# Five dense chunks at the head of the value pass, and the list constants on GpSimd in three blocks

## The chip, the cores and the metric

The kernel runs on one core of a Trainium2 chip. The metric is the device time of one launch in microseconds (us), the median of the runs shown. Five engines work side by side, each on its own queue in order: PE (matmuls), DVE (vector), ACT (activations and casts), POOL (GpSimd; here it also issues every indirect DMA) and SP (issues plain DMAs). The profile's names for them are used throughout; PEld is PE's weight load.

## The reference

A decoder trunk of two layers on 256 tokens of width 1024. Each layer is a token mixer (mLSTM in layer 0, RG-LRU in layer 1) with a memory cross-attention beside it, a layer norm, and then a channel mixer called PEER, whose second half is what matters here. PEER scores 128 x 128 = 16384 experts by products of two keys, keeps 16 experts for each of 8 heads and each token, and computes

```python
u = u_tab[eid]
act = jax.nn.gelu(jnp.einsum('nhkd,nd->nhk', u, xb).astype(jnp.float32), approximate=False)
coef = (gw * act).astype(x.dtype)
return jnp.einsum('nhk,nhkd->nd', coef, v_tab[eid])
```

A second layer norm follows. All arrays are float32.

## The kernel before

**Precision.** Every large product is made of three matmuls (`mm3`, lines 253 to 257): operands are split into a high part (a cast on ACT, line 153 for weights, 310 for coefficients) and a low part (a subtraction, line 163, 166 or 168 on POOL or DVE for weights, 311 on DVE for coefficients), and high x high, high x low and low x high are added in PSUM. The split of weights is called `wH`, `wL`; that of coefficients `cH`, `cL`. Both have rings of three buffers (`HL_BUFS`), so the cast for one chunk waits until PE has finished the chunk three places ahead of it.

**PEER as dense tables.** The 16384 experts lie in 128 chunks of 128. In the U pass, `u_step` multiplies chunk after chunk of the U table with all 256 tokens (24 matmuls of 128x256 in each step); GELU and the routing weights give a coefficient for each expert and token, in the tiles `lo` (chunks 0 to 47, tile name `wglo`) and `hi` (chunks 48 to 127, `wghi`). The first 48 steps run beside the routing, the next 64 beside the building of the routing weights, and the last 16 (`h` = 64 to 79, lines 1450 to 1467) beside a generator, `tail_lists`, that is advanced once for each step.

**Lists.** Of chunks 0 to 103 (`NJ` = 104) few rows matter, since each token uses 128 experts. `lists` (from line 1079) finds for each of the 128 partitions which chunks hold a used expert, and packs the used rows into 54 columns: 16 + 5 that matter only for the first block of 128 tokens, 16 + 6 only for the second, and 11 for both (columns 21 to 31). The results are `vrow` (`vids`: which rows of the V table a column needs) and `crow` (which rows of the coefficients, which the kernel dumps to a DRAM tensor `rows`, line 1073). The first 11 of its pieces are eleven `tensor_reduce` on DVE, counted by `tick`; at tick 4, POOL makes index constants (lines 1120 to 1137) in a part of `lo` that is free by then. Chunks 104 to 127 are dense: all their rows are used, and their coefficients are on the chip.

**Value pass.** It adds up 78 items: 24 dense chunks and 54 sparse columns. For an item of both blocks of tokens PE runs 12 matmuls of 128x512, for a column of one block 6. `value_order` (lines 66 to 86) fixes the order of the items from three numbers: it models that the first column can be multiplied at `FIRST_US`, one more every `PAIR_US`, that a dense item takes `ITEM_US`, and places dense chunks wherever a column would still be late. The last 3 items of layer 0 and the last 6 of layer 1 are kept apart and multiplied for the first block of tokens, then for the second.

**What a column needs.** A dense chunk is loaded by SP (line 200) into one of 5 `raw` buffers, or into one of 9 further buffers of the same size that come free in the pass (`ahead` in `wghi`, and `slots`). A column needs two indirect DMAs that POOL issues (line 205): a gather of 128 rows of V (512 KB) into such a buffer, and a gather of its coefficient rows (`wghi<-rows,crow`) into `hi`. As soon as `vids` is there, `begin` (line 208) issues gathers for the first five columns, and `coef_rows` (line 1436) issues coefficient gathers up to ten items ahead, four at a time. All of it stands in POOL's one queue in program order. `load` (line 176) takes the items in order and stops at a column while `vids` is not known.

The numbers behind the order:

```python
FIRST_US, PAIR_US, ITEM_US = 5.0, 2.8, 2.73
...
        while dense and t < FIRST_US + k * PAIR_US:
            out.append((dense.pop(0), None))
            t += ITEM_US
        t = max(t, FIRST_US + k * PAIR_US) + ITEM_US * len(blocks(c)) / 2
```

With them the order of layer 0 begins D D 21 0 D 1 2 D 3 22 (D a dense chunk, a number a column).

Of the kernel before, what the change touches and what calls it, by code (L numbers as in the profile page):

```python
# [39 lines left out]
COLS = A_END + SIDE + SPILLS[1]  # L40
WIDTH = 57
NC = P - NJ + COLS
FIRST_US, PAIR_US, ITEM_US = 5.0, 2.8, 2.73
SLOTS = 4
CLASS = 128.0
SKEW = 3
# [49 lines left out]
class Trunk:  # L96
# [982 lines left out]
    def lists(self, layer):  # L1079
        nc = self.nc  # L1080
# [3 lines left out]
        def take(*shape, dt=F32):  # L1084
            n = math.prod(shape)
            w = n if dt is not F16 else (n + 1) // 2
            v = words[:, at[0]:at[0] + w]
            at[0] += w
            assert at[0] <= 20 * T
            v = v if dt is F32 else v.bitcast(dt)  # L1090
            if len(shape) == 2:
                v = v.rearrange("p (a b) -> p a b", a=shape[0])
            return v
# [6 lines left out]
        pi, qi, ti, zi = take(3, NJ, dt=I32), take(2, dt=I32), take(4, dt=I32), take(SPILL, dt=I32)  # L1100
        jv, pq, tv, zv = take(3, NJ), take(4), take(4), take(SPILL)
# [15 lines left out]
        for tick, g in enumerate(g for g in range(NJ // 8) if g not in ACT_GROUPS):  # L1117
            nc.vector.tensor_reduce(mB[:, 8 * g:8 * g + 8], self.part_of(8 * g, 8, 1), axis=AX.X, op=ALU.max,
                                    apply_absolute_value=True)
            if tick == 4:  # L1120
                g_ = nc.gpsimd
                g_.iota(pi, pattern=[[int(CLASS), 3], [1, NJ]], base=1, channel_multiplier=0)
                g_.iota(qi, pattern=[[-P, 2]], base=1, channel_multiplier=1)
                g_.iota(ti, pattern=[[int(CLASS), 4]], base=0, channel_multiplier=0)
                g_.iota(zi, pattern=[[P, SPILL]], base=0, channel_multiplier=0)
                g_.tensor_copy(jv, pi)
                g_.tensor_copy(pq[:, 0:2], qi)
                for c in (1, 2):
                    g_.tensor_scalar(pq[:, 1 + c:2 + c], pq[:, 1:2], -CLASS * P * c, None, op0=ALU.add)
                g_.tensor_copy(tv, ti)  # L1130
                g_.tensor_copy(zv, zi)
                g_.memset(one, 1.0)
                g_.affine_select(tri, one, pattern=[[1, P]], base=0, channel_multiplier=-1,
                                 compare_op=ALU.is_gt, fill=0.0)
                g_.memset(ones, 1.0)
                for c in range(3):
                    g_.memset(zoff[:, first[c]:first[c + 1]], -P - CLASS * P * c)
            if tick == 8:
                b = self.bank()
                jp, tp = b[:, :3 * NJ].rearrange("p (a b) -> p a b", a=3), b[:, 3 * NJ:3 * NJ + 4]  # L1140
                nc.scalar.copy(jp, jv)
                nc.scalar.copy(tp, tv)
            yield 1.15
# [120 lines left out]
    def peer_layer(self, layer):  # L1264
        nc, tc, A = self.nc, self.tc, self.A
        with ExitStack() as ctx:
# [123 lines left out]
            def tail_lists():  # L1390
                lists = self.lists(layer)
                marks = [c for g in ACT_GROUPS for c in range(8 * g, 8 * g + 8)]
                budget, n = 0.0, 0
                while True:
                    gain = LIST_US if self.vrow is None else REST_US
                    budget = min(budget + gain, gain)
                    if n < NJ // 8:
                        self.dump(nc.scalar, 8 * DUMPS[n], 8, CUT, T)
                    while lists and budget > 0:
                        c = next(lists, -1.0)  # L1400
                        if c is None:
                            break
                        if c < 0:
                            lists = None
                            break
                        budget -= c
                    for _ in range(3):
                        if marks:
                            self.used(marks.pop(0), 1)
                    self.marked = not marks  # L1410
                    self.dumped = n >= NJ // 8 - 1
                    self.listed = not lists
                    n += 1
                    yield
# [286 lines left out]
```

## Time and profile before

| | |
|---|---|
| median of 3 runs | 1483.71 us (1479.94 to 1486.09) |
| the profiled execution: time, span | 1483.08 us, 1481.3 us |
| PE busy | 1438.8 us (97% of the span) |
| DVE, ACT, POOL busy | 1191.7, 892.2, 683.1 us |
| last 16 U steps | about 544 to 588 us in layer 0, 1262 to 1306 us in layer 1 |
| value pass on PE | 588.49 to 752.3 us in layer 0, 1306.49 to 1473.2 us in layer 1 |
| indirect DMAs issued by POOL | 108 in each layer |

Times in the profile are microseconds from the start of the span. A timeline row gives start, duration, engine, line, operation, the tile written and the tiles read, and in brackets how long the engine sat idle ahead of it and what ended the wait ("issue" means nothing that the profile shows). A row with "x6" merges six instructions that follow one another. A waits row gives the total of the waits, how many there were, and the longest. A windows row gives the stretch, its length, the busy time and count of each engine asked for, the granted TensorE clock as a share of full speed, the busy share of the DMA engines and GB/s.

### The profile page before, as it was taken

How to read it: one execution, taken by the hardware profiler on the slowest of the kernel's cores; microseconds unless marked ns; L12 is line 12 of the kernel's file. 1: busy time of each engine (PE TensorE's matmuls, PEld its weight loads, DVE VectorE, ACT ScalarE, POOL GpSimd, SP SyncE). 2: the span in 40 equal slices, each digit the busy share in tenths (PEclk: the TensorE clock that was granted, in tenths of full speed). 3: DMA queues.
4: the chain of work that ended last, by engine and by line, in shares of the span. 5: the costliest groups of instructions: out<-in, count | busy, mean ns of one | idle time of the engine just before them, and what ended most of it. 6: DMA issues, size and time to landing. Idle time of an engine off the chain costs nothing.

```text
span 1481.3 us, 30314 instructions
## 1 busy us (share of the span) xinstructions
PE 1438.8 (97%) x11173; PEld 1355.4 (91%) x11173; DVE 1191.7 (80%) x2688; ACT 892.2 (60%) x1895; POOL 683.1 (46%) x571
## 2 busy tenths in 40 slices
PE   9999999999999999899999999999999999989997
PEld 8998999999999999688899789999999999978885
DVE  4677377989999998687886855979899999777777
ACT  5555455455559984477756645555455798636664
POOL 2202578213333348777710166732333333877772
PEclk9999999999999999999999999999999999999999
DMA  7645655555548999889855255555555799988982
GB/s 235 228 141 172 202 172 185 186 179 163 167 161 270 263 244 279 305 291 324 285 203 176 72 174 171 173 186 171 185 158 164 225 277 259 257 301 286 312 282 87
DMA packets 165787, 317.41 MB, mean 214 GB/s; under 512 B 65245, under 2 KB 94946, under 8 KB 165378
## 3 DMA queue, kind: packets, MB, share of 16 engines
q1 hardware_dynamic: 90552, 226.68, 47.5%
q0 software_dynamic: 19360, 65.16, 13.1%
q10 hardware_dynamic: 55722, 23.60, 6.0%
q8 instruction: 88, 1.44, 0.4%
q14 instruction: 65, 0.53, 0.1%
HBM read 287.07 MB, written 28.32 MB: 213 GB/s over the span
## 4 chain that ended last, share of the span: by engine, by line
PE 35%; issue 5%; POOL 4%; DVE 3%; DMA 3%; ACT 1%; DVEq 0%; POOLq 0%; ACTq 0%
PE bank L255 11%; PE bank L257 11%; PE bank L256 11%; POOL wghi L205 2%; PE bank L1374 2%; DMA wghi<-in_v_dram,vids 1%; DMA wghi<-rows,crow 1%; DVE wL L168 1%; POOL raw L205 1%; PE bank L314 1%; DMA slots<-in_v_dram,vids 1%; POOL slots L205 0%; DVE xc L829 0%; ACT pr L545 0%; ACT wH L153 0%
## 5 line engine op out<-in xcount | busy, mean ns | idle before, releaser
L255 PE MATMUL bank<-xHL,wH 128*128 128x256 f32 x2536 | 716.8, 283 | 1.8 <-ACT wH L153 1.8
L257 PE MATMUL bank<-xHL,wL 128*128 128x256 f32 x2536 | 706.5, 279 | 9.1 <-DVE wL L168 6.2
L256 PE MATMUL bank<-xHL,wH 128*128 128x256 f32 x2536 | 704.6, 278 | 2.3 <-DVE xHL L311 2.2
L153 ACT CAST wH<-raw 128x1024 fp32r<-128x1024 f32 (+3 forms) x409 | 421.6, 1032 | 392.1 <-PE bank L256 124.1
L257 PEld LDWEIGHTS bank<-xHL,wL 128*128 128x128 f32 x2536 | 476.4, 188 | 13.3 <-DVE wL L168 9.1
L255 PEld LDWEIGHTS bank<-xHL,wH 128*128 128x128 f32 x2536 | 477.6, 188 | 3.0 <-ACT wH L153 2.8
L256 PEld LDWEIGHTS bank<-xHL,wH 128*128 128x128 f32 x2536 | 477.3, 188 | 3.1 <-DVE xHL L311 3.1
L166 POOL TENSOR_TENSOR wL<-raw,wH 128x1024 fp32r<-128x1024 f32 (+1 forms) x123 | 271.1, 2210 | 193.9 <-ACT wH L153 191.7
L168 DVE TENSOR_TENSOR wL<-raw,wH 128x1024 fp32r<-128x1024 f32 (+3 forms) x194 | 210.4, 1090 | 146.7 <-ACT wH L153 144.6
L163 POOL TENSOR_TENSOR wL<-raw,wH 128x386 fp32r<-128x386 f32 x128 | 131.4, 1027 | 285.4 <-DVE wL L161 285.4
L255 PE MATMUL bank<-wH,cH 128*128 128x512 f32 (+1 forms) x443 | 174.7, 394 | 12.3 <-ACT cH L310 12.0
L257 PE MATMUL bank<-wH,cL 128*128 128x512 f32 (+1 forms) x443 | 174.1, 393 | 0.0
L256 PE MATMUL bank<-wL,cH 128*128 128x512 f32 (+1 forms) x443 | 173.8, 392 | 0.0
L1027 DVE TENSOR_TENSOR oh<-iota,i12T 128x1024 f16<-128x1024 f16 x128 | 136.3, 1065 | 0.0
L205 POOL DMA_INDIRECT wghi<-rows,crow x108 | 118.6, 1098 | 32.9 <-issue 30.8
L255 PEld LDWEIGHTS bank<-wH,cH 128*128 128x128 f32 x443 | 84.4, 191 | 31.7 <-ACT cH L310 13.7
L161 DVE TENSOR_TENSOR wL<-raw,wH 128x640 fp32r<-128x640 f32 x128 | 105.5, 824 | 9.1 <-ACT wH L153 3.2
L257 PEld LDWEIGHTS bank<-wH,cL 128*128 128x128 f32 x443 | 84.2, 190 | 18.4 <-DVE cL L311 0.6
L256 PEld LDWEIGHTS bank<-wL,cH 128*128 128x128 f32 x443 | 84.3, 190 | 17.8 <-DVE wL L168 0.2
L1030 DVE TENSOR_TENSOR oh<-oh,gT 128x1024 f16<-128x1024 f16 x128 | 90.0, 703 | 4.4
L168 DVE TENSOR_TENSOR wL<-wghi,wH 128x1024 fp32r<-128x1024 f32 x56 | 68.5, 1223 | 25.0 <-ACT wH L153 25.0
L153 ACT CAST wH<-wghi 128x1024 fp32r<-128x1024 f32 x56 | 58.8, 1050 | 36.9 <-PE bank L257 35.7
(373 smaller groups left out, 2017.6 us busy)
## 6 DMA issues: line engine op xcount, KB each, us to landing
raw<-in_u_dram SPq DMA_DIRECT2D x256, 512.0 KB, 3.4
raw<-in_w_q_dram SPq DMA_DIRECT2D x32, 512.0 KB, 3.8
raw<-in_v_dram SPq DMA_DIRECT2D x21, 512.0 KB, 4.8
wghi<-in_v_dram SPq DMA_DIRECT2D x17, 512.0 KB, 4.8
raw<-in_w_out_dram SPq DMA_DIRECT2D x16, 512.0 KB, 3.8
rows<-wghi ACTq DMA_DIRECT2D x14, 512.0 KB, 5.7
rows<-wglo ACTq DMA_DIRECT2D x12, 512.0 KB, 4.4
slots<-in_v_dram SPq DMA_DIRECT2D x10, 512.0 KB, 6.0
```

The lines of the kernel that those rows point to most:

```text
L153: (nc.vector.tensor_copy if self.cast_dve else nc.scalar.copy)(h[:, c], r[:, c])
L161: nc.vector.tensor_sub(l[:, k:], r[:, k:], h[:, k:].bitcast(F32))
L163: nc.gpsimd.tensor_sub(l[:, :k], r[:, :k], h[:, :k].bitcast(F32))
L166: nc.gpsimd.tensor_sub(l[:, :k], r[:, :k], h[:, :k].bitcast(F32))
L168: nc.vector.tensor_sub(l[:, k:], r[:, k:], h[:, k:].bitcast(F32))
L205: self.nc.gpsimd.indirect_dma_start(out=dst, out_offset=None, in_=table, in_offset=bass.IndirectOffsetOnAxis(ap=rows, axis=0))
L255: mm(out, sH, mH, start=start, stop=False, skip_group_check=True)
L256: mm(out, sH, mL, start=False, stop=False, skip_group_check=True)
L257: mm(out, sL, mH, start=False, stop=stop, skip_group_check=True)
L1027: nc.vector.tensor_tensor(flat(oh[:, 1:3]), self.iota2.unsqueeze(1).to_broadcast([P, 4, P, 2]), pairs(self.i12T[:, j]), op=ALU.is_equal)
L1030: nc.vector.tensor_tensor(flat(oh[:, 0:2]), two.rearrange("p z (q e t) -> p z q e t", q=2, t=2), pairs(self.gT[:, j]), op=ALU.mult)
L1374: nc.tensor.matmul(wp[:, qs], oh[:, 2, q // 2, :, q % 2], oh[:, z, q // 2, :, q % 2], start=z == 0, stop=z == 1, skip_group_check=True)
```

## The change

Two constants of `value_order` are new, and POOL's constants for the lists are made at ticks 4, 6 and 8 in place of all at tick 4. Two ticks fall in one U step, so the three blocks stand beside three U steps that follow one another.

```diff
-FIRST_US, PAIR_US, ITEM_US = 5.0, 2.8, 2.73
+FIRST_US, PAIR_US, ITEM_US = 13.0, 2.65, 2.73
...
+            g_ = nc.gpsimd
             if tick == 4:
-                g_ = nc.gpsimd
                 g_.iota(pi, pattern=[[int(CLASS), 3], [1, NJ]], base=1, channel_multiplier=0)
+                g_.iota(ti, pattern=[[int(CLASS), 4]], base=0, channel_multiplier=0)
+                g_.tensor_copy(jv, pi)
+                g_.tensor_copy(tv, ti)
+            if tick == 6:
                 g_.iota(qi, pattern=[[-P, 2]], base=1, channel_multiplier=1)
-                g_.iota(ti, pattern=[[int(CLASS), 4]], base=0, channel_multiplier=0)
                 g_.iota(zi, pattern=[[P, SPILL]], base=0, channel_multiplier=0)
-                g_.tensor_copy(jv, pi)
                 g_.tensor_copy(pq[:, 0:2], qi)
                 for c in (1, 2):
                     g_.tensor_scalar(pq[:, 1 + c:2 + c], pq[:, 1:2], -CLASS * P * c, None, op0=ALU.add)
-                g_.tensor_copy(tv, ti)
                 g_.tensor_copy(zv, zi)
+            if tick == 8:
                 g_.memset(one, 1.0)
```

The order of layer 0 now begins D D D D D 21 0 D 1 2 D 3 22. The three dense chunks come from later places: the dense chunk behind column 5, one behind column 37 and one behind column 20 are gone from there. From column 48 on the two orders are the same, and so is the amount of work: 24 dense chunks, 54 columns, 678 matmuls in each layer's pass.

POOL's queue in the last U steps of layer 0, before (`wL<-raw,wH` is the subtraction of one U step, `wglo` the place of the constants):

```order
L166 TENSOR_TENSOR wL<-raw,wH 128x1024 x3
L1122 IOTA wglo 128x312
L1123 IOTA wglo 128x2
L1124 IOTA wglo 128x4
L1125 IOTA wglo 128x14
L1126 CAST wglo<-wglo 128x312
...
L1133 AFFINE_SELECT wglo<-wglo 128x128
...
L1137 MEMSET wglo 128x3
L166 TENSOR_TENSOR wL<-raw,wH 128x1024 x10
```

and now, at the same place:

```order
L166 TENSOR_TENSOR wL<-raw,wH 128x1024 x3
L1122 IOTA wglo 128x312
L1123 IOTA wglo 128x4
L1124 CAST wglo<-wglo 128x312
L1125 CAST wglo<-wglo 128x4
L166 TENSOR_TENSOR wL<-raw,wH 128x1024
L1127 IOTA wglo 128x2
...
L1132 CAST wglo<-wglo 128x14
L166 TENSOR_TENSOR wL<-raw,wH 128x1024
L1134 MEMSET wglo 128x128
...
L1139 MEMSET wglo 128x3
L166 TENSOR_TENSOR wL<-raw,wH 128x1024 x8
```

Thirteen subtractions stand there in both (3 + 10, and 3 + 1 + 1 + 8); two of them have moved ahead of parts of the constants. Some rows of constants are left out of both.

POOL's queue behind it, where the gathers of layer 0 begin, before (`vids` gathers fetch V rows, `crow` gathers coefficient rows):

```order
L205 DMA wghi<-in_v_dram,vids 128x1024 x5
L205 DMA raw<-in_v_dram,vids 128x1024
L205 DMA wghi<-rows,crow 128x256
L205 DMA wghi<-rows,crow 128x128 x3
L205 DMA raw<-in_v_dram,vids 128x1024
L205 DMA wghi<-rows,crow 128x128
```

and now:

```order
L205 DMA wghi<-in_v_dram,vids 128x1024 x5
L205 DMA wghi<-rows,crow 128x256
L205 DMA wghi<-rows,crow 128x128 x3
L205 DMA slots<-in_v_dram,vids 128x1024 x4
L205 DMA raw<-in_v_dram,vids 128x1024
L205 DMA wghi<-rows,crow 128x128
```

The first coefficient gather is now the sixth of the queue, where it was the seventh; the number of gathers is 108 in both.

ACT's queue at the head of the value pass of layer 0, before (`wH` is the cast of an item, `cH` that of its coefficients two items ahead of PE):

```order
L1455 ACTIVATE bank<-bank 128x256 x2
L153 CAST wH<-wghi 128x1024
L310 CAST cH<-wghi 128x256
L153 CAST wH<-wghi 128x1024
L310 CAST cH<-wghi 128x128
```

and now:

```order
L1457 ACTIVATE bank<-bank 128x256 x2
L153 CAST wH<-raw 128x1024
L310 CAST cH<-wghi 128x256
L153 CAST wH<-raw 128x1024
L310 CAST cH<-wghi 128x256
L153 CAST wH<-raw 128x1024
L310 CAST cH<-wghi 128x256
L153 CAST wH<-wghi 128x1024
L310 CAST cH<-wghi 128x256
L153 CAST wH<-wghi 128x1024
L310 CAST cH<-wghi 128x128
```

Three pairs of casts for dense chunks (`wH<-raw`, whose coefficients lie on the chip) now stand ahead of the first pair that needs gathered data. Lines behind 1137 are two higher in the changed kernel.

## Prediction

> **What bounds the kernel now.** I read the page's chain of work that ended last first, then PE's waits around the two value passes, then the timelines at the waits, and then POOL's row of gathers.
>
> ```profile
> PE 35%; issue 5%; POOL 4%; DVE 3%; DMA 3%; ACT 1%; DVEq 0%; POOLq 0%; ACTq 0%
> ```
>
> PE leads the chain, but POOL has more of it than any other engine, and that is not POOL's arithmetic: it is the gathers of the value passes. PE's waits in the last U steps and the value pass of layer 0, and then in those of layer 1:
>
> ```profile
> PE bank L255 <- ACT cH L310: 5.8, 1, 5.8
> PE bank L257 <- POOL wL L166: 1.2, 1, 1.2
> ```
>
> ```profile
> PE bank L255 <- ACT cH L310: 6.2, 3, 5.4
> ```
>
> So there are two waits for each layer that the change aims at. The larger one in PE's timeline, in layer 0, in layer 1, and then an undisturbed stretch at the end of layer 0's pass:
>
> ```profile
> 593.75 0.39 PE L257 MATMUL bank<-wH,cL 128*128 128x512 f32 x1
> 599.93 0.80 PE L255 MATMUL bank<-wH,cH 128*128 128x512 f32 x1 [5.80 <-ACT cH L310]
> 605.16 0.40 PE L255 MATMUL bank<-wH,cH 128*128 128x512 f32 x1
> ...
> 1311.75 0.39 PE L257 MATMUL bank<-wH,cL 128*128 128x512 f32 x1
> 1317.57 0.79 PE L255 MATMUL bank<-wH,cH 128*128 128x512 f32 x1 [5.43 <-ACT cH L310]
> 1321.95 0.39 PE L256 MATMUL bank<-wL,cH 128*128 128x512 f32 x1
> ...
> 743.16 0.39 PE L257 MATMUL bank<-wH,cL 128*128 128x512 f32 x1
> 744.07 0.39 PE L255 MATMUL bank<-wH,cH 128*128 128x512 f32 x1
> 744.52 0.39 PE L257 MATMUL bank<-wH,cL 128*128 128x512 f32 x1
> ...
> 752.07 0.40 PE L257 MATMUL bank<-wH,cL 128*128 128x512 f32 x1
> ```
>
> At full speed one matmul follows the other after 1.36 / 6 = 0.227 us (743.16 to 744.52). PE stops after the two dense items at 593.75, and goes on 6.18 us later, 5.95 more than a step. The next 12 matmuls take 5.23 us (599.93 to 605.16) where 2.72 is normal, since the granted clock is down:
>
> ```profile
> 600.00:610.00 10.00, 10.00 (x34) 8.04 (x35) 8.64 (x13) 5.29 (x9) 7.96 (x7) 0.75 0.82 283
> ```
>
> That is 2.51 more, 8.46 us in layer 0. In layer 1 it is 5.59 for the stop and 4.38 - 2.27 = 2.11 for ten slow matmuls, 7.70 us. What it waits for is the first coefficient gather, and ACT shows that:
>
> ```profile
> 599.48 0.40 ACT L310 CAST cH<-wghi 128x256 fp32r<-128x256 f32 x1 [9.47 <-DMA wghi<-rows,crow]
> ```
>
> Now POOL, which issues that gather. First gather, first coefficient gather, gathers inside PE's stop, and the last two of layer 0; then the same places of layer 1, with the last row and the one for the last single-block column (1445.88); and the busy time of POOL alone in both stretches, 108 gathers in each:
>
> ```profile
> 583.06 1.16 POOL L205 DMA_INDIRECT wghi<-in_v_dram,vids  x1 [2.37 <-DVE wglo L1213]
> 591.87 1.78 POOL L205 DMA_INDIRECT wghi<-rows,crow  x1 [0.30 <-issue]
> 593.96 0.95 POOL L205 DMA_INDIRECT wghi<-rows,crow  x1 [0.30 <-issue]
> 600.21 0.95 POOL L205 DMA_INDIRECT wghi<-rows,crow  x1 [0.30 <-issue]
> ...
> 736.05 1.83 POOL L205 DMA_INDIRECT wghi<-rows,crow  x1 [0.30 <-issue]
> 738.18 0.95 POOL L205 DMA_INDIRECT wghi<-rows,crow  x1 [0.30 <-issue]
> ...
> 1301.02 1.04 POOL L205 DMA_INDIRECT wghi<-in_v_dram,vids  x1 [2.34 <-DVE wglo L1213]
> 1311.94 0.95 POOL L205 DMA_INDIRECT wghi<-rows,crow  x1 [0.30 <-issue]
> 1445.88 0.94 POOL L205 DMA_INDIRECT wghi<-rows,crow  x1 [0.30 <-issue]
> 1449.88 1.05 POOL L205 DMA_INDIRECT wghi<-rows,crow  x1 [0.30 <-issue]
> ```
>
> ```profile
> 583.00:740.00 157.00, 122.83 (x108) 0.98 0.87 300
> 1301.00:1451.00 150.00, 117.29 (x108) 0.98 0.87 295
> ```
>
> 122.83 us of gathers and about 108 gaps of 0.30 (32.4) fill 155 of the 157 us; 117.29 + 32.4 fill all of layer 1's 150. POOL never rests in the value pass. The row of gathers lasts from 583.06 to 739.13 and from 1301.02 to 1450.93, through PE's stop, and its end is not set by PE. That is the fact on which the forecast turns: PE's last items need the last gathers.
>
> How near PE is to them at the end: time from issue to landing of the gathers issued from 734 to 740, and of those from 1445 to 1451, and PE's waits in layer 1 there:
>
> ```profile
> DMA to landing us min/median/max: 3.7/3.7/4.9
> ```
>
> ```profile
> DMA to landing us min/median/max: 5.7/6.7/7.7
> ```
>
> ```profile
> 1451.07 0.50 PE L255 MATMUL bank<-wH,cH 128*128 128x512 f32 x1 [0.59 <-ACT cH L310]
> 1452.90 0.50 PE L255 MATMUL bank<-wH,cH 128*128 128x512 f32 x1 [0.15 <-ACT cH L310]
> ```
>
> In layer 1 PE already waits a little for the last single-block columns: the gather at 1445.88, fourth from the end of POOL's row, is that of column 53 and serves the matmul at 1452.90, 7.02 us later (counted along POOL's gathers and PE's items), which is landing (6.7) and a cast. Slack there: none. In layer 0 the last but one gather (736.05), that of column 30, serves the item at 744.07, 8.02 us later. It needs 4.9 at most to land and some 0.8 for the cast and the subtraction (0.40 in ACT's row above, as much again on DVE), 5.7 in all. Slack there: 2.3, or 3.5 with the landing of 3.7. I take 2.6.
>
> **The change part by part.** *The five dense chunks.* They give PE 5 x 12 x 0.227 = 13.6 us before the first column, so it is wanted at 588.49 + 13.6 = 602.1. Its gather is now sixth in POOL's queue, some 1.3 us earlier; even at the old time its cast stood at 599.48 and PE could go at 599.93. The stop goes, with the slow clock behind it: 8.46 and 7.70 us, 16.16 in all. The loads of the three chunks cost nothing that I can find: SP issued the fourth dense load ahead of any gather,
>
> ```profile
> 580.72 0.33 SPq L200 DMA_DIRECT2D raw<-in_v_dram  x1
> ```
>
> and the first four of the five are these same loads. The fifth takes the buffer of the last U chunk, at about 585, and is wanted 588.49 + 10.9 = 599.4. If the landings get slower for it, there are 2 us before the first column is late.
>
> What is late next? Behind column 20 the order is the old one, so PE would come to the last columns 8.46 (7.70) us earlier, with the gathers where they are. It has 2.6 us of slack there in layer 0, none in layer 1. The rest of the 16.16 us is waited for again, in pieces of about one gather each, from the middle of the pass to its end. Gain from this part: 2.6 and 0.
>
> *The gathers' own pace.* The six inside PE's stop (593.96 to 600.21, and 1311.94 on) took 0.95, against 122.83 / 108 = 1.137 and 117.29 / 108 = 1.086 on average. When PE stands still DVE does too, and the gathers are shorter; beside DVE's work they are longer, as the one at 591.87 (1.78 us) beside this:
>
> ```profile
> 592.14 0.69 DVE L1234 TENSOR_TENSOR wglo<-iota,wglo 128x512 f16<-128x512 f16 x1
> ```
>
> With the stop filled, six gathers take the average: 6 x 0.19 = 1.1 and 6 x 0.14 = 0.8 us lost. The bounds are wider than that. Layer 0's 107 steps from first to last took 155.1 us and layer 1's 148.9 for the same work, so the pace differs by 6.2 us for reasons of which gather meets which DVE instruction; the change moves all of them. I take the loss and keep 6.2 us either way, for each layer, for the range.
>
> The Trainium skill, "SBUF — State Buffer", section "Who interferes with whom", says that a DVE `tensor_tensor` takes only the read side of the port shared with GpSimd, and infers that descriptor generation, which needs the write side, is not held up by it. The gather of 1.78 us beside a tensor_tensor speaks against it here; by the page these 1.9 us would not be lost, and the time below would be 1.9 us shorter.
>
> *The constants in three blocks.* POOL and PE around them:
>
> ```profile
> 553.05 0.40 POOL L1122 IOTA wglo<- 128x312 int32 x1
> ...
> 555.65 14.20 POOL L166 TENSOR_TENSOR wL<-raw,wH 128x1024 fp32r<-128x1024 f32 x6
> ```
>
> ```profile
> 554.80 0.28 PE L255 MATMUL bank<-xHL,wH 128*128 128x256 f32 x1
> ...
> 556.61 0.28 PE L256 MATMUL bank<-xHL,wH 128*128 128x256 f32 x1
> 558.08 0.39 PE L257 MATMUL bank<-xHL,wL 128*128 128x256 f32 x1 [1.19 <-POOL wL L166]
> ```
>
> The block takes 555.65 - 553.05 = 2.60 us and each subtraction 14.20 / 6 = 2.37. A U step takes 24 x 1.81 / 16 = 2.72 (554.80 to 556.61 is 16 matmuls). PE wanted the next low part one matmul after 556.61, at 556.73; POOL had it at 555.65 + 2.37 = 558.02, and PE went on at 558.08, 1.35 late. In three blocks the same 2.60 us is spread over three subtractions, and POOL gains 2.72 - 2.37 = 0.35 in each step. The third is done at 553.05 + 2.60 + 3 x 2.37 = 562.76, and wanted at 556.73 + 2 x 2.72 = 562.17. So 0.6 is still lost and 0.75 gained, in each layer. Bounds: 0, if POOL's lag is only moved, and 1.35. What is queued behind the blocks on POOL are subtractions of the next steps, and only PE waits for these; the copy of the index constants on ACT comes at tick 8, behind the first block as before. As the U steps come earlier, so do the lists and the first gather (583.06): the row of gathers moves by the same 0.75.
>
> **Sum**, against the profiled execution's 1483.08 us. Layer 0: slack 2.6, plus 0.75, minus 1.1: 2.25 gained. Layer 1: 0 + 0.75 - 0.8: nothing. Together some 2.2 us, 1480.9. The median of the runs is 0.6 above the profiled one, so I predict 1481.5 as the median. By the bounds: landing (2.3 or 3.5), constants (0 to 1.35 twice) and pace (6.2 either way; both layers seldom the same way) give 1474 to 1488 for this case alone.
>
> **The rivals.** *The whole wait is won.* If the row of gathers is no limit, because gathers get shorter when PE runs evenly, 16.2 + 1.5 us are gained: 1483.7 - 17.7 = 1466.0. For it speaks the size of the stop, and that the profile shows no other of PE in these passes before their last columns. Against it: the gathers end at 1450.93 whatever PE does, and PE waits for them there already. For all of it the 108 gathers would have to take 0.94 each (0.94 + 0.30 is 134 us), and only those did that ran beside an idle DVE. Half way is possible, with layer 0 at layer 1's pace.
>
> *The clock goes down again at the end of the pass.* PE's new waits stand near the last columns. If they are long enough for the clock to halve, the items behind them run slowly, and no gather hides the last ones. One such stretch cost 2.51 and 2.11 us. With one more in each layer where the forecast has none: 1481.5 + 4.6 = 1486.1, slower than before by 2.4. It decides at a wait between 1.19 us, which left PE's pace alone at 558.08, and 5.43, which did not. For it: 8 us have to be waited for somewhere. Against it: gathers come 1.25 to 1.5 us apart, so each wait should be about that. In the Trainium skill, "TensorE: Matmul & The Clock Gate", section "Why this matters for your kernels", gaps under about 3 us between bursts keep the clock; by that rule waits of 1.5 us cost no speed.
>
> *The stop stays.* If three more early loads delay the coefficient gather by over 2 us, PE only stops later and for less time; with the gathers as the limit this costs little, and the constants remain: 1483.7 - 1.5 = 1482.2. Against it: four of the five loads were early already.
>
> **How the numbers follow.** About 0.5%, 7.4 us, is what a measurement of this kernel can tell from no change. The forecast, gathers as the limit: 0.64, of which 0.12 is faster by more than 7.4 (a better pace in both layers) and 0.02 slower by more. The whole wait, or most of it, won: 0.18, all faster. The clock again: 0.10, of which 0.03 over 7.4 slower, where the pace is bad too. The stop stays: 0.08, of which 0.01 slower. Faster 0.30, same 0.64, slower 0.06. The range has to take in part of the second case: 1470 leaves out 0.14 of it, and 1488 leaves out 0.06 above.
>
> **What would show it.** In the changed kernel's timeline, PE goes from U steps into five dense items and the first column with no wait over 1 us, and the granted clock stays at 1.00 there. POOL's 108 gathers stand 0.30 us apart again and last 150 to 157 us. PE's waits for `cH` (line 310) are many, around 1 us each, in the last third of both passes, and sum to some 5 us in layer 0 and 8 in layer 1. The wait for `wL` at the constants is about 0.6 us. The forecast is wrong if POOL has gaps in its row, if the row gets shorter by more than 6 us, or if PE ends the pass without waits.

## The result and the profile after

| | before | changed |
|---|---|---|
| median of 8 runs each | 1483.82 us (1479.94 to 1486.09) | 1493.18 us (1485.84 to 1501.21) |
| ratio, 95% interval | | 1.0067 (1.0044 to 1.0090) |
| the profiled execution: time, span | 1483.08 us, 1481.3 us | 1493.1 us, 1491.4 us |

The change makes the kernel slower by 0.67%, 9.4 us. The forecast was 1481.5 us, in a range of 1470 to 1488, so it had the sign wrong, and the median lies outside the range.

The stop that the change was aimed at is gone. PE's waits in the last U steps and the value pass of layer 0, from 535 to 770 us, and then those of layer 1, from 1260 to 1491 (source and releaser, total, count, longest):

```profile
PE bank L256 <- DVE wL L168: 4.5, 9, 0.8
PE bank L255 <- ACT cH L310: 1.7, 2, 1.1
PE bank L255 <- ACT wH L153: 0.6, 1, 0.6
PE bank L257 <- POOL wL L166: 0.3, 1, 0.3
...
PE bank L255 <- ACT cH L310: 8.7, 8, 2.8
PE bank L256 <- DVE wL L168: 1.2, 4, 0.3
```

The longest wait left is 2.8 us. Waits have come back in small pieces, 7.1 us in layer 0 and 9.9 in layer 1. The wait for the constants (`POOL wL`) fell from 1.2 to 0.3 and 0.2 us. At the head of layer 0's pass PE is busy throughout, at full clock (PE's busy time and count, granted clock, DMA share, GB/s):

```profile
590.00:600.00 10.00, 10.00 (x46) 1.00 0.97 369
600.00:610.00 10.00, 10.00 (x70) 1.00 0.83 254
```

PE's first wait in this pass is at 614.93, of 0.64 us. So the work that DVE has to do at the head doesn't hold PE up there.

The loss is in POOL's row of gathers. Its busy time in the two stretches that hold the 108 gathers of a layer:

```profile
581.00:742.00 161.00, 126.98 (x108) 1.00 0.88 296
1304.00:1462.00 158.00, 124.20 (x108) 1.00 0.85 282
```

The gathers took 126.98 us where it had been 122.83, and 124.20 where it had been 117.29: 4.15 and 6.91 us more for the same 108 gathers. POOL's timeline shows where: the first gather, the sixth to the eighth, and the last of each layer.

```profile
581.94 1.16 POOL L205 DMA_INDIRECT wghi<-in_v_dram,vids  x1 [2.37 <-DVE wglo L1215]
589.47 1.00 POOL L205 DMA_INDIRECT wghi<-rows,crow  x1 [0.30 <-issue]
590.76 6.84 POOL L205 DMA_INDIRECT wghi<-rows,crow  x1 [0.30 <-issue]
597.91 0.98 POOL L205 DMA_INDIRECT wghi<-rows,crow  x1 [0.30 <-issue]
...
740.74 1.04 POOL L205 DMA_INDIRECT wghi<-rows,crow  x1 [0.30 <-issue]
1304.72 1.04 POOL L205 DMA_INDIRECT wghi<-in_v_dram,vids  x1 [2.35 <-DVE wglo L1215]
1312.27 1.00 POOL L205 DMA_INDIRECT wghi<-rows,crow  x1 [0.30 <-issue]
1313.57 6.84 POOL L205 DMA_INDIRECT wghi<-rows,crow  x1 [0.30 <-DMA wghi<-in_v_dram,vids]
1320.71 0.99 POOL L205 DMA_INDIRECT wghi<-rows,crow  x1 [0.30 <-issue]
...
1460.59 0.95 POOL L205 DMA_INDIRECT wghi<-rows,crow  x1 [0.31 <-issue]
```

One gather in each layer, the seventh of the row and the second that fetches coefficients, took 6.84 us. No gather before had taken over 2.46. Layer 0's row begins 1.12 us earlier than before and ends 2.65 later (741.78 against 739.13); layer 1's begins 3.70 later and ends 10.61 later (1461.54 against 1450.93). The span is 10.1 us longer. ACT shows that PE now depends on this row: its `cH` casts waited for a coefficient gather 12 times in layer 0, 24.5 us in all (before: once, 9.5 us), and 26 times in layer 1, 39.9 us (before: 3 times, 11.5 us).

The same duration to a hundredth of a microsecond in both layers does not look like a landing or a queue that fills. DVE's timeline beside the gather in layer 0 (a row "x2" merges two instructions):

```profile
589.55 0.42 DVE L1458 TENSOR_TENSOR wghi<-wghi,bank 128x256 f32<-128x256 f32 x1
589.88 1.22 DVE L168 TENSOR_TENSOR wL<-raw,wH 128x1024 fp32r<-128x1024 f32 x1
591.01 0.69 DVE L1236 TENSOR_TENSOR wglo<-iota,wglo 128x512 f16<-128x512 f16 x1
591.61 0.42 DVE L311 TENSOR_TENSOR cL<-wghi,cH 128x256 fp32r<-128x256 f32 x1
591.95 1.23 DVE L168 TENSOR_TENSOR wL<-raw,wH 128x1024 fp32r<-128x1024 f32 x1
593.08 1.30 DVE L1236 TENSOR_TENSOR wglo<-iota,wglo 128x512 f16<-128x512 f16 x2
594.29 0.43 DVE L311 TENSOR_TENSOR cL<-wghi,cH 128x256 fp32r<-128x256 f32 x1
594.62 1.23 DVE L168 TENSOR_TENSOR wL<-raw,wH 128x1024 fp32r<-128x1024 f32 x1
595.76 0.69 DVE L1236 TENSOR_TENSOR wglo<-iota,wglo 128x512 f16<-128x512 f16 x1
596.36 0.43 DVE L311 TENSOR_TENSOR cL<-wghi,cH 128x256 fp32r<-128x256 f32 x1
596.86 1.23 DVE L168 TENSOR_TENSOR wL<-wghi,wH 128x1024 fp32r<-128x1024 f32 x1
```

Compare each row's end with the next row's start. From 589.88 to 596.79 DVE never pauses: every instruction starts 0.08 to 0.10 us before the recorded end of the one ahead of it. At 596.79 (596.36 + 0.43) the first true pause begins, of 0.07 us. The gather ends at 597.60, 0.81 after that. Before the change, the same place in DVE's row was followed by PE's stop; this is the next DVE row after the one at 592.14 that the prediction shows:

```profile
599.91 0.43 DVE L311 TENSOR_TENSOR cL<-wghi,cH 128x256 fp32r<-128x256 f32 x1 [7.08 <-ACT cH L310]
```

DVE paused there at 592.83, and the gather of 1.78 us issued at 591.87 ended at 593.65, 0.82 after it. So both kernels have a gather that waits for DVE's first pause. PE's stop had supplied the pause at once; without the stop it comes 6 us later.

An ordinary gather waits for less. DVE and then POOL, further on in layer 0 of the changed kernel:

```profile
616.04 1.23 DVE L168 TENSOR_TENSOR wL<-slots,wH 128x1024 fp32r<-128x1024 f32 x1 [0.84 <-ACT wH L153]
617.18 0.42 DVE L311 TENSOR_TENSOR cL<-wghi,cH 128x256 fp32r<-128x256 f32 x1
617.52 1.22 DVE L168 TENSOR_TENSOR wL<-slots,wH 128x1024 fp32r<-128x1024 f32 x1
```

```profile
616.44 1.65 POOL L205 DMA_INDIRECT wghi<-rows,crow  x1 [0.30 <-issue]
618.40 1.17 POOL L205 DMA_INDIRECT wghi<-rows,crow  x1 [0.30 <-issue]
```

The first started while the subtraction of 616.04 ran, and ended at 618.09, 0.82 after that subtraction's end (617.27), though DVE went straight on. The second started 0.88 us into the subtraction of 617.52 and ended at 619.57, 0.83 after it (618.74). Counted over both kernels and both layers, 279 of the 432 gathers started at least 0.05 us into a `tensor_tensor` of DVE that had more than 0.12 us to go. In 272 of them the duration is that rest plus 0.82, within 0.05 us. The seven others are two firsts of a row and the five that were held past the end of the running instruction (1.78, 1.76 and 2.46 us before, 6.84 twice after). The other 153 took 0.94 us in the median, and all but 4 of them at most 1.06; among them are 12 that started within 0.04 us of the start of a `tensor_tensor` and were not delayed.

### The profile page after: what moved, and what is told of

Read it like the earlier page. It is cut to its first block, busy times and chain, and to the rows that moved or that the text cites. A ratio compares the mean times of both kernels' runs of the same rounds, so it can differ in the third digit from the quotient of the medians.

```text
span 1491.4 us, 30296 instructions
## 1 busy us (share of the span) xinstructions
PE 1445.6 (97%) x11173; PEld 1352.3 (91%) x11173; DVE 1192.7 (80%) x2688; ACT 890.7 (60%) x1895; POOL 694.3 (47%) x571
## 4 chain that ended last, share of the span: by engine, by line
PE 64%; DMA 13%; POOL 7%; DVE 7%; issue 6%; ACT 3%; SPq 0%; ACTq 0%; DVEq 0%; POOLq 0%
PE bank L255 19%; PE bank L257 19%; PE bank L256 19%; DMA wghi<-rows,crow 5%; PE bank L1376 4%; DMA wghi<-in_v_dram,vids 3%; POOL wghi L205 3%; DVE wL L168 3%; PE bank L314 2%; DMA slots<-in_v_dram,vids 2%; ACT wH L153 1%; POOL wL L166 1%; POOL slots L205 1%; POOL raw L205 1%; DMA raw<-in_v_dram 1%
## 5 line engine op out<-in xcount | busy, mean ns | idle before, releaser
L205 POOL DMA_INDIRECT wghi<-rows,crow x108 | 133.2, 1233 | 32.9 <-issue 29.0
L310 ACT CAST cH<-wghi 128x128 fp32r<-128x128 f32 (+1 forms) x156 | 53.2, 342 | 72.3 <-DMA wghi<-rows,crow 64.4
```

Of the source, the lines that this page charges most:

```text
L205: self.nc.gpsimd.indirect_dma_start(out=dst, out_offset=None, in_=table, in_offset=bass.IndirectOffsetOnAxis(ap=rows, axis=0))
```

## The experiments

The theory: one gather in each layer is held until DVE's first true pause, the five dense chunks take that pause away, and since the gathers are a row without gaps, all that stands behind is late by it. The main rival at this point was a full queue: seven gathers of up to 512 KB are under way beside two dense loads, and POOL must wait for a landing.

The experiments ran on chips on which the kernel before takes 1523 to 1531 us, not 1484, and POOL's row has gaps, up to 7.7 us long. Most of them end with one of DVE's subtractions, which frees a buffer. So times are compared only within a set of runs made together on one chip (a "call" in the expectations), and every ratio is to the kernel before in the same set.

**First set: the change taken apart, and the one-hot pieces moved.** The constants alone: the changed kernel with `FIRST_US` and `PAIR_US` put back.

```diff
-FIRST_US, PAIR_US, ITEM_US = 13.0, 2.65, 2.73
+FIRST_US, PAIR_US, ITEM_US = 5.0, 2.8, 2.73
```

> Only the constants in three blocks; the value pass opens with two dense chunks as before. Theory (one coefficient gather, the seventh of POOL's row, is held for 6.84 us by an unbroken row of DVE instructions in each layer of the changed kernel, and the row of gathers sets the end): the stop of PE at the head of the value pass stays at 5 to 6 us, so DVE runs dry there and the seventh gather takes about 1.8 us as before; the wait for wL at the constants falls from 1.2 to 0.2 us, the row of gathers starts about 1 us earlier in each layer, and the time falls by about 2 us, 1481.5 to 1482.5. Rival (the constants themselves, or the earlier start of the lists, bring the loss): 1490 or more, with a gather of several us in the row here too.

Measured: 0.9985 of before (0.9960 to 1.0010). PE's stop is there in both layers (5.7 us in layer 0), the waits for the constants are 0.2 us each, and the seventh gather took 1.78 and 1.77 us. POOL, and the DVE row whose end (594.13) let it go 0.83 us before its own:

```profile
593.18 1.78 POOL L205 DMA_INDIRECT wghi<-rows,crow  x1 [0.30 <-issue]
```

```profile
593.45 0.68 DVE L1236 TENSOR_TENSOR wglo<-iota,wglo 128x512 f16<-128x512 f16 x1
```

The constants bring no loss. The interval holds the expected gain of 2 us, and also no change.

The order alone: the kernel before, with its constants in one block, and

```diff
-FIRST_US, PAIR_US, ITEM_US = 5.0, 2.8, 2.73
+FIRST_US, PAIR_US, ITEM_US = 13.0, 2.65, 2.73
```

> Only the five dense chunks; the constants in one block as before. Theory (DVE's unbroken row holds the seventh gather, and the five dense chunks make the row unbroken): the seventh gather takes 6 to 7 us in both layers, and the time is that of the changed kernel plus the 2 us of the constants, 1494 to 1496. Rival (the long gather needs the shift of the lists by the three blocks as well): the seventh gather takes under 2 us and the time is 1480 to 1485.

Measured: 1.0027 (0.9999 to 1.0055). The seventh gather in layer 0 and in layer 1:

```profile
589.04 6.84 POOL L205 DMA_INDIRECT wghi<-rows,crow  x1 [0.31 <-issue]
...
1335.46 6.84 POOL L205 DMA_INDIRECT wghi<-rows,crow  x1 [0.31 <-issue]
```

The held gather belongs to the five dense chunks. The time came out lower than expected: 1494 to 1496 us of 1483.8 would be 1.007 to 1.008, above the interval.

The changed kernel with the one-hot pieces four items later (line 1236, DVE's rows `wglo<-iota,wglo`, which compare numbers to build one-hot tables for the lists' last columns):

```diff
+        for _ in range(4):
+            yield None
         for r in range(0, OVER, 4):
```

> The changed kernel, with the one-hot pieces of the lists (128x512, line 1236) four value items later. Theory (DVE's unbroken row from the first one-hot on holds the gather): after the subtraction that runs when the seventh gather starts, DVE pauses for its cast, so this gather takes 0.34 + 0.82 = 1.2 us instead of 6.84; the row of gathers gets 5.7 us shorter in each layer, and the time falls by about 11 to 1482 (1479 to 1485). Rival (POOL's queue is full: seven gathers are under way beside two dense loads, and the eighth must wait for a landing): the seventh gather stays at 6 to 7 us and the time at 1493.

Measured: 0.9945 (0.9906 to 0.9984). The time fell by more than expected (1479 to 1485 us would be 0.997 to 1.001), though the interval reaches into that. The seventh gather took 1.49 us in both layers. The duration expected was 1.2: DVE did not pause at the end of the running subtraction, but one instruction later, as the same place in a later run of this kernel shows (e12_late, POOL and then DVE):

```profile
591.87 1.50 POOL L205 DMA_INDIRECT wghi<-rows,crow  x1 [0.30 <-issue]
```

```profile
590.99 1.22 DVE L168 TENSOR_TENSOR wL<-raw,wH 128x1024 fp32r<-128x1024 f32 x1
592.13 0.41 DVE L311 TENSOR_TENSOR cL<-wghi,cH 128x256 fp32r<-128x256 f32 x1
592.55 1.23 DVE L168 TENSOR_TENSOR wL<-raw,wH 128x1024 fp32r<-128x1024 f32 x1
```

The row at 592.13 ends at 592.54, the next starts at 592.55, and 592.54 + 0.82 is 593.36; the gather ended at 593.37. Gathers of 512 KB and dense loads stand around it as in the changed kernel, so a full queue is not what held it.

One one-hot piece for each item, so that the pause comes half way:

```diff
                 q16[:, r:r + 4].unsqueeze(2).to_broadcast(full), op=ALU.is_equal)
-            yield 0.7
+            yield 1.0
```

> The changed kernel, with one one-hot piece (line 1236) per value item instead of one, two, one, one, two. Theory (a true pause of DVE lets the held gather go, 0.82 us before its end): the second item's coefficient subtraction must wait for its cast, DVE pauses some 3.0 us after the gather's start, and the seventh gather takes 3.0 + 0.82 = 3.8 us instead of 6.84; each row gets 3 us shorter, and the time is about 1487 (1484 to 1490). Rival (POOL's queue is full until a landing): 6 to 7 us and 1493.

Measured: 1.0008 (0.9974 to 1.0042). The seventh gather took 4.17 and 4.16 us, against 3.8 expected. In layer 0 (POOL, DVE):

```profile
593.71 4.17 POOL L205 DMA_INDIRECT wghi<-rows,crow  x1 [0.30 <-issue]
```

```profile
596.03 0.68 DVE L1236 TENSOR_TENSOR wglo<-iota,wglo 128x512 f16<-128x512 f16 x1
596.63 0.42 DVE L311 TENSOR_TENSOR cL<-wghi,cH 128x256 fp32r<-128x256 f32 x1
597.10 1.23 DVE L168 TENSOR_TENSOR wL<-raw,wH 128x1024 fp32r<-128x1024 f32 x1
```

The pause is at 597.05, the gather's end at 597.88, 0.83 later. So the held gather's length follows DVE's first pause: 1.5, 4.2 and 6.8 us for pauses 0.7, 3.3 and 6.0 us after its start, and 0.82 or 0.83 remains each time. The row did not get the expected 3 us shorter, though: all 216 gathers together took 258.9 us here against 251.0 in the order alone, so others got longer. Of the times of this set, only e3_late is clear of no change.

**Second set: what the held gather costs, and what sets it off.** The changed kernel itself, and the late pieces again (no new edit):

> The changed kernel itself again, beside the other kernels of this call. Both theories: the seventh gather takes 6.84 us in both layers; 0.3 to 0.9% slower than before.

> The changed kernel with the one-hot pieces four value items later once more, now beside the changed kernel. Theory (the held gather is the whole loss): the seventh gather takes 1.5 us, and the time is 10 to 11 us under that of the changed kernel, a little under before (0.997 to 1.000 of it) where the gathers are issued back to back. Rival (the held gather is only made up for by other waits later, and the loss lies in the tail of the pass): within 4 us of the changed kernel.

Measured: 1.0045 (1.0018 to 1.0073) for the changed kernel, 0.9974 (0.9951 to 0.9996) with the pieces late, where the seventh gather took 1.50 and 1.49 us. The profiled execution of e5_changed took 5095 us, so its rows are not read. The difference is 0.71% of 1523, 10.8 us, known by the two intervals to some 5 us either way. Two gathers that are 6.84 - 1.49 = 5.35 us shorter make 10.7, which fits. The rival's bound of 4 us lies just outside.

Late pieces, and the subtractions of the value pass in two halves:

```diff
-                nc.vector.tensor_sub(l[:, k:], r[:, k:], h[:, k:].bitcast(F32))
+                halves = (k, n) if self.vrow is None or k or n < D else (0, D // 2, D)
+                for b, e in zip(halves, halves[1:]):
+                    nc.vector.tensor_sub(l[:, b:e], r[:, b:e], h[:, b:e].bitcast(F32))
```

> The kernel with the late one-hot pieces, and each 128x1024 subtraction of the value passes on DVE (line 168, 1.23 us) as two of 128x512. Theory (a gather that starts while such a subtraction runs waits for its end): the mean gather falls from 1.13 to about 1.04 us, the rows get 8 to 10 us shorter, and PE's waits in the last third go; up to 10 us faster than the kernel with late one-hot pieces alone, if DVE's added 0.1 us per item does not make DVE the limit. Rival (the gathers do not set the end of the pass): within 2 us of it, or slower by DVE's added work.

Measured: 1.0035 (1.0009 to 1.0062), slower than the late pieces alone by 0.6%. The gathers did get shorter, from 122.9 to 117.1 us in layer 0 and from 121.7 to 115.8 in layer 1, less than the 8 to 10 us expected. But POOL's waits grew: the gaps over 0.5 us in its row add up to 25.3 us in layer 0 and 19.2 in layer 1, against 8.7 and 10.1 in e6_late. One of them, 6.2 us in layer 0, is a wait for the lists (line 1253), which come later with the late pieces. Two halves of a subtraction take 1.37 us on DVE (2 x 686 ns) where the whole takes 1.22, too little to explain 9 us. Why this kernel is slower stays open.

Six small memsets on POOL between the second and the third gather:

```diff
+            if len(self.slots) == wait == AHEAD - 2:
+                for _ in range(6):
+                    self.nc.gpsimd.memset(self.rest, 0.0)
```

> The changed kernel with six small memsets on POOL between its second and third gather, which start every later gather of the row some 0.6 to 1 us later against DVE. Theory A (whichever gather starts about 0.9 us into the subtraction ahead of the one-hot pieces is held): the seventh gather is no longer the one held, and either none or another one takes several us. Theory B (it is the seventh of the row, whatever DVE is at): the seventh is held until DVE's next true pause, 5 to 6 us.

Measured: one run, 1544.08 us, which says nothing of the time. Now the sixth gather is held in both layers, 6.87 us, and the seventh takes 0.95. POOL and DVE in layer 0:

```profile
597.51 6.87 POOL L206 DMA_INDIRECT wghi<-rows,crow  x1 [0.30 <-issue]
604.68 0.95 POOL L206 DMA_INDIRECT wghi<-rows,crow  x1 [0.30 <-issue]
```

```profile
596.64 1.22 DVE L169 TENSOR_TENSOR wL<-raw,wH 128x1024 fp32r<-128x1024 f32 x1
...
603.13 0.42 DVE L317 TENSOR_TENSOR cL<-wghi,cH 128x256 fp32r<-128x256 f32 x1
603.58 1.22 DVE L169 TENSOR_TENSOR wL<-wghi,wH 128x1024 fp32r<-128x1024 f32 x1
```

The gather starts 0.87 us into the subtraction, as the seventh did in the changed kernel (590.76 - 589.88 = 0.88), and ends 0.83 after the pause at 603.55. Theory A holds: it is the place in DVE's row that decides, not the place in POOL's.

The moment alone doesn't decide: the gather of 618.40 above started just as far into a subtraction and was not held. The traces show one difference, in the instruction ahead of the subtraction. Over all fifteen traces that can be read, 366 gathers started 0.86 to 0.89 us into one of DVE's long subtractions. In 22 of them the instruction ahead was the multiplication of line 1458 (the row at 589.55 above; 1456, 1460 or 1464 in the other kernels), which reads a `bank` of PSUM: all 22 were held past the end of the subtraction. In the other 344 it was another one, line 311 in nearly all, and none was held. No run changes this instruction alone, so whether it is the cause stays open.

**Third and fourth set: the comparison again, and an earlier row.** The late pieces (e9, e12) and the changed kernel (e11, e13), unedited, and the late pieces with

```diff
-LIST_US, REST_US, LOOK = 2.25, 1.0, 10
+LIST_US, REST_US, LOOK = 3.0, 1.0, 10
```

> The changed kernel with the one-hot pieces four value items later, a third time. Theory (the held gather is the whole loss of the change): 0.7% under the changed kernel; where POOL issues its gathers back to back, 0.997 to 1.000 of before. Rival (the gain seen so far comes from the chip's slower loads): as the changed kernel where POOL issues back to back.

> As the kernel with late one-hot pieces, and the lists are made at a budget of 3.0 us for each U step instead of 2.25, so that the first gather is issued one U step (2.7 us) earlier. Theory (the row of gathers sets the end of the pass): 2 to 5 us faster than the kernel with late one-hot pieces alone, for two layers, if no gather is held anew. Rival (landings, or PE, set the end): within 2 us of it.

> The changed kernel itself, for comparison with the two others of this call. Both theories: the seventh gather takes 6.84 us in both layers, 0.3 to 0.9% slower than before.

> The changed kernel with the one-hot pieces four value items later. Theory (the held gather is the whole loss): 0.4 to 0.8% under the changed kernel of this call; if POOL issues back to back here, 10 to 11 us under it and 0.997 to 1.000 of before. Rival (where POOL issues back to back the loss lies in the tail of the pass): within 4 us of the changed kernel there.

> The changed kernel itself, for comparison. Both theories: 0.3 to 0.9% slower than before; the seventh gather takes 6.84 us in the layers where it starts 0.87 to 0.89 us into DVE's subtraction, and under 2 us where it starts elsewhere.

> The kernel with late one-hot pieces and the lists at 3.0 us for each U step. Theory (the row of gathers sets the end of the pass): 2 to 5 us faster than the kernel with late one-hot pieces alone. Rival (landings or PE set the end): within 2 us of it.

| | third set | fourth set |
|---|---|---|
| late pieces | 0.9975 (0.9939 to 1.0011) | 0.9948 (0.9922 to 0.9974) |
| late pieces, lists earlier | 0.9973 (0.9939 to 1.0006) | 0.9977 (0.9952 to 1.0002) |
| changed | 1.0012 (0.9979 to 1.0045) | 1.0022 (0.9992 to 1.0053) |

The late pieces stand 0.37% and 0.74% under the changed kernel, 5.7 and 11.3 us, each known to some 6 or 7 us. In e13_changed the seventh gather took 6.85 and 6.83 us. In e11_changed's profiled execution only layer 1's was held; POOL's seventh gather of layer 0 and, farther on, of layer 1:

```profile
592.44 0.95 POOL L205 DMA_INDIRECT wghi<-rows,crow  x1 [0.30 <-issue]
...
1341.50 6.83 POOL L205 DMA_INDIRECT wghi<-rows,crow  x1 [0.30 <-issue]
```

In layer 0 loads came late there, DVE had paused ahead of this gather, and no gather of the layer met the moment. So the same kernel pays the cost in one layer and not in the other; that this set's difference is half that of the others fits, but one profiled execution doesn't show it for all runs.

The earlier lists moved the first gather of the fourth set by 3.3 and 1.7 us (579.78 against 583.05, 1316.31 against 1317.98), and the expected 2 to 5 us were not seen: the ratio is the same in the third set and 0.29% higher in the fourth. The third set is too uncertain to exclude 2 us (by its medians, 1521.82 against 1530.57 us, the earlier lists would even be 9 us faster). So that an earlier start of the row brings an earlier end on these chips is not shown. That the 10.8 us of the held gathers come through, and these 5 us do not, is not explained by any run here.

The late pieces have a price of their own. The lists' last columns depend on the one-hot pieces, and in 4 of the 10 layers profiled with late pieces (the halves included) POOL's row has a gap that ends with a row of these lists, of 0.8 to 7.7 us. None of these sets ran on a chip where POOL issues back to back, so what the late pieces are worth there was not seen; the working below puts the held gathers at 11 us, and such waits would go off that.

The late pieces beat both kernels: in all four sets below before (0.9945, 0.9974, 0.9975, 0.9948, three of them clear of 1), and below the changed kernel in the three that had it. Five dense chunks and constants in three blocks together with the late pieces are worth about 0.4% on these chips.

## Why the prediction was wrong

**The step that failed** is "the gathers' own pace": "With the stop filled, six gathers take the average: 6 x 0.19 = 1.1 and 6 x 0.14 = 0.8 us lost." The gathers took 4.15 and 6.91 us more. The stop did not only let six gathers be short. It was the pause of DVE for which the gather at 591.87 waited. Layer 0's row got 159.84 - 156.07 = 3.77 us longer and layer 1's 156.82 - 149.91 = 6.91; a held gather costs 6.84 - 1.16 = 5.68 over one let in at the end of the running subtraction. Without it the rows would have been 1.9 us shorter and 1.2 us longer, inside the bounds of 6.2 that the prediction set. The row needed was at hand: the prediction quotes 1.78 us at 591.87 and DVE's instruction at 592.14, and reads them as "beside DVE's work they are longer". Put end to end they say more: the gather ended 0.82 us after DVE's last instruction ahead of a pause of 7.08 us. The question that was not asked is what ends that gather when the pause goes.

**The range failed with it.** It took the two layers' pace as two draws ("both layers seldom the same way"). The held gather is no draw: on that chip both layers run the same code in the same rhythm, and both paid 5.68 us, 11.4 in all. The span grew by 10.1, so without them it would have been 1.3 us shorter, where the forecast was 2.2. That is worked out, not measured.

**What was right.** PE goes into the five dense chunks without a stop, with the granted clock at 1.00. POOL's gathers are the limit on that chip: they stand 0.30 us apart, and what PE no longer waits at the head it waits later. In layer 1 the waits for `cH` are 8.7 us, forecast 8. In layer 0 they are 1.7 instead of 5; 4.5 us went instead into waits for `wL` from DVE, which the prediction did not name. Two of these at least (617.32 and 741.02) are gather waits at second hand: an ACT cast ahead of DVE's subtraction had waited for a coefficient gather. The row of 150 to 157 us was missed in layer 0 (159.84) and just kept in layer 1 (156.82).

**The slack** of 2.6 us that the prediction gave PE at the end of layer 0 was not seen. The row ends 2.65 us later, and PE's pass ends 2.46 later (754.93 against 752.47). PE's last wait in it is at 741.02, for a column ahead of the one on which the prediction had counted the slack (that of the last gather but one).

**The constants** were mis-sized to the safe side: the wait fell by 0.9 and 1.0 us (1.2 to 0.3 and 0.2), forecast 0.75, and the first gather of layer 0 came 1.12 us earlier.

**The rivals.** The whole wait was not won, and the stop did not stay. The clock did go down at the end of the pass, once, in layer 1. PE's longest wait there, and PE's busy time, matmuls and granted clock in the next 4.5 us:

```profile
1462.33 0.50 PE L255 MATMUL bank<-wH,cH 128*128 128x512 f32 x1 [2.84 <-ACT cH L310]
```

```profile
1463.00:1467.50 4.50, 4.50 (x14) 0.62 0.02 5
```

A clock of 0.62 over 4.5 us is 0.38 x 4.5 = 1.7 us lost. So that rival held in one layer, for about 1.7 of the 2.1 to 2.5 us that it was priced at, and it is not the main loss. In the Trainium skill, "TensorE: Matmul & The Clock Gate", section "Why this matters for your kernels", idle gaps over about 3 us are the ones to avoid; here a wait of 2.84 us was followed by the drop. PE had been busy for only 4.11 of the 8 us from 1455 to 1463, and whether the smaller waits count as well no run here shows.

**The sentence on the port.** The prediction weighed "SBUF — State Buffer", section "Who interferes with whom", of the Trainium skill, by what that page infers: that a `tensor_tensor` leaves descriptor generation alone. The 272 gathers that ended 0.82 us after the running `tensor_tensor` speak against this for a whole gather. The same section also states that a DVE instruction with two SBUF inputs contends with a GpSimd instruction that reads SBUF. A gather takes its row numbers from `vids` or `crow` in SBUF, so that rule would fit a wait at the gather's start; no run here tells which of its accesses waits.

## What to carry to other kernels

When a stall is removed, list who else worked in it: here POOL's gather got its turn because DVE stood still, and filling the stall turned 1.8 us into 6.8 in a row where every microsecond counts. Before trusting a mean duration, line up one instruction's end with the neighbour's end: a constant remainder (0.82 us here) shows a wait, and whom it waits for. Pieces of work with time to spare, as the one-hot pieces, belong away from the stretch in which another engine needs gaps, but not so far that their own results come late.

## What the runs showed of the hardware

- A gather of 128 rows keeps POOL busy for 0.94 us where DVE leaves it alone, with 0.30 us to the next, and it makes no difference whether its rows are 512 KB or 64 KB together. If it starts at least 0.05 us into a DVE `tensor_tensor` with more than 0.12 us to go, it ends 0.82 us after that instruction's end (272 of 279). The mean gather before took 1.14 us in layer 0 and 1.09 in layer 1 for that reason.
- A gather can miss the turn at the end of the running instruction. The seventh then got in only when DVE paused; pauses of 0.01 to 0.10 us were enough, and it took 1.5, 4.2 or 6.8 us by where the first of them lay. DVE instructions that follow one another without a gap overlap in the records by 0.08 to 0.10 us; in e6_late an overlap of only 0.02 us was enough. The gather of 2.46 us is another case: later ones like it (2.36 us in e9_late) got in where the overlap was 0.08.
- All 22 gathers that started 0.86 to 0.89 us into a long subtraction directly behind a DVE multiplication that reads PSUM were held; of the 344 at the same moment behind other instructions, none was. That is seen, not tested.
- The held gather took 6.83 to 6.85 us all seven times that it was the seventh of the row, in four profiled executions with loads at different times, which speaks against a wait for memory.
